# The x buffers hold x only, and the squares for the next block's norm are queued in the middle of a block

## The chip, the cores and the metric

The kernel runs on one core of a Trainium2 chip. The metric is the device time of one execution in microseconds (us); the number compared is the median of several runs. Profiles come from one profiled execution; its span runs from the first to the last instruction.

Engines are named as the profile names them: PE is TensorE (matrix products), PEld its weight loads, DVE is VectorE, ACT is ScalarE, POOL is GpSimd, and SP is the engine whose queue issues all of this kernel's DMAs.

## The reference

One layer of a streaming encoder, for a prompt of 2048 frames (behind 16 learned meta tokens) and a sample of 32 frames with a cache of 528 rows:

```
n  = rmsnorm(x, norm_g)                          # x * rsqrt(mean(x^2) + eps) * g, width 1024
q, k, v, z_a, b_g, c_g, u, z_c = split(n @ w_in) # 8 groups of 512 columns
# attention, 4 heads, chunk-causal, with relative position bias:
a  = softmax(q1 k1 / 8 + bias) - lambda * softmax(q2 k2 / 8 + bias)
o  = rmsnorm(a @ v, subln_g) * (1 - lambda_init) * silu(z_a)
# short convolution of width 3:
yc = silu(z_c) * b_g * conv3(c_g * u)
y  = rmsnorm(x + concat(o, yc) @ w_out, final_g)
```

It also returns k, v and the last two rows of the convolution's input. All of it is in 32-bit floats; the kernel splits each operand of a large product in a high and a low part and multiplies three times.

## The kernel before

The prompt is worked through in four blocks of 512 frames (p = 0 to 3); block 0 carries the meta tokens and the sample as well. For each block, x arrives transposed (features on the partitions) in eight tiles `xt`, and ScalarE and VectorE write from each a high part `xh` and a low part `xl`, already times the norm's weight (`x_load`, L141 to L174). The rest of the norm, the factor 1/sqrt(mean of squares) of each frame, is multiplied in when a projection leaves its accumulator (`rbs[p]`, L254, L280, L305, L352 and the like).

That factor is made apart. `x_stats(p + 1)` (L108) loads x once more, with the frames on the partitions, in eight tiles `xr` of 128 by 512. ScalarE squares each and sums it along its row (L115), and a few tiny instructions turn the sums into the factor r (L117, L178 to L184). `x_rms` (L121) spreads r along a diagonal (`dg`, VectorE, L127) and multiplies it with a matrix of ones (`pb`, TensorE, L129), so that every partition holds the factor of every frame; ScalarE copies that into the tile rb (L130). These three are traced at a high priority.

Within a block, four units h = 0 to 3 follow each other. `unit_a(h, p)` (L237) projects q, k, v and the gate z of one head; `attend(h, p, st)` (L432) makes the scores, softmax and outputs; `unit_c(u, p)` makes a quarter of the convolution branch. In blocks 0 to 2 no convolution unit follows h = 3. A projection is 24 products (L225) into an accumulator of the ring pj, which has two buffers; the block's first projection of q, the product `pb` and the transposes of v share that ring. Each projection's weights are loaded (`wr`), cast by ScalarE to a high part (L204) and their low part is made by GpSimd or VectorE (L78).

`unit_a` writes, in this order, the g tiles `q32`, `k32`, `v32t`, `v32`, `z32` and `l1`. The last two are written behind the last projection, z: the eviction L352 writes `z32`, and `softplus_neg` (L188 to L191) writes `l1`. The casts of k that `ev_k` makes for the score products are L285; there are two in blocks 1 to 3 and four in block 0.

Buffers come from rings of a fixed number of tiles with the same tag. The two that matter here:

- The tag xt, eight tiles of 128 by 512 (`XB = 8`). It holds the eight `xr`, the diagonal `dg`, the eight `xt`, in block 0 also the cached keys and values of the sample (`kts` and `cvt`, two per head), and in block 3 some others.
- The tag g, eight tiles of 128 by 564 (`g_tile`). It holds the short-lived tiles of the units, and later those of the output stage.

The order of the instructions on each engine and on the DMA queue isn't written out. A scheduler works it out ahead of time with a simulated timeline: at each moment an engine takes, of the instructions that are ready, the one with the highest priority, which is the one traced first unless it is marked. On the chip each engine then runs its list in that order. `x_stats(p + 1)` is traced behind `unit_a(2, p)`, and `x_rms` and `x_load(p + 1)` behind `unit_a(3, p)`:

```
st = unit_a(h, p)
if h == 2 and p < NQ - 1:
    r = x_stats(p + 1)
...
if h == H - 1 and p < NQ - 1:
    x_rms(p + 1, r)
    x_load(p + 1)
attend(h, p, st)
```

After the four blocks comes an output stage of 17 tiles (`out_first`, `out_rest`).

Of the kernel before, what the change touches and what calls it, by code (L numbers as in the profile page):

```python
# [11 lines left out]
F32 = mybir.dt.float32  # L12
# [5 lines left out]
P = 128  # L18
# [9 lines left out]
QT = 512  # L28
# [7 lines left out]
XB = 8  # L36
# [11 lines left out]
def hybrid_step(ctx: ExitStack, tc: tile.TileContext, x, xT, ckT, cv, scT, rel_bias, norm_g, w_in,  # L48
# [13 lines left out]
    one = pool("one", 1)  # L62
# [6 lines left out]
    V, S, G, T = nc.vector, nc.scalar, nc.gpsimd, nc.tensor  # L69
# [3 lines left out]
    def halved(out, a, b, op, engine=None):  # L73

        n = out.shape[-1] if len(out.shape) == 2 else out.shape[1]
        cuts = (0, n // 2, n) if engine is None and n * (out.shape[-1] if len(out.shape) > 2 else 1) > 256 else (0, n)
        for c0, c1 in zip(cuts, cuts[1:]):
            (engine or G).tensor_tensor(out[:, c0:c1], a[:, c0:c1], b[:, c0:c1], op=op)  # L78

    dma = lambda out, in_: nc.sync.dma_start(f32(out), f32(in_))  # L80
    g_tile = lambda n=564: gp.tile([P, 564], F32, tag="g", name="g")[:, :n]
# [26 lines left out]
    def x_stats(p):  # L108

        ssq = sm.tile([P, 8], F32, tag="ssq", name="ssq", bufs=1)  # L110
        for j in range(8):
            xr = one.tile([P, QT], F32, tag="xt", name="xr", bufs=XB)
            r0 = NX + QT * p + P * (j // 2)
            dma(xr, x[r0:r0 + P, 512 * (j % 2):512 * (j % 2) + 512])
            S.activation(xr, xr, AF.Square, accum_out=ssq[:, j:j + 1])  # L115
        ssp, var, r, w = (sm.tile([P, 4], F32, tag=f"x{i}", name=f"x{i}", bufs=1) for i in range(4))
        V.tensor_reduce(ssp, ssq.rearrange("p (t i) -> p t i", i=2), op=ALU.add, axis=AX.X)  # L117
        rsqrt(r, ssp, var, w, 1.0 / D)
        return r

    def x_rms(p, r):  # L121

        rb = one.tile([P, NX + QT], F32, tag="rb", name="rb")
        pb = ps_j.tile([P, 512], F32, tag="pj", name="pb")
        dg = one.tile([P, QT], F32, tag="xt", name="dg", bufs=XB)
        with tc.high_priority():
            V.tensor_tensor(by_tile(dg), ident.unsqueeze(1).broadcast_to([P, 4, P]),  # L127
                            r.unsqueeze(2).broadcast_to([P, 4, P]), op=ALU.mult)
            T.matmul(pb, lhsT=ones, rhs=dg, start=True, stop=True)  # L129
            S.copy(rb[:, :QT], pb)  # L130
        rbs[p] = rb
# [44 lines left out]
    def rsqrt(r, ssum, var, w, scale):  # L176

        V.tensor_scalar(var, ssum, scale, EPS, op0=ALU.mult, op1=ALU.add)  # L178
        S.activation(r, var, AF.Ln)
        S.activation(r, r, AF.Exp, scale=-0.5)  # L180
        V.tensor_tensor(w, r, r, op=ALU.mult)
        V.tensor_tensor(w, w, var, op=ALU.mult)
        V.tensor_scalar(w, w, -0.5, 1.5, op0=ALU.mult, op1=ALU.add)
        V.tensor_tensor(r, r, w, op=ALU.mult)  # L184
# [52 lines left out]
    def unit_a(h, p):  # L237
# [5 lines left out]
        st = {}  # L243
# [21 lines left out]
        for c in range(2):  # L265
            r, o = slice(64 * c, 64 * c + 64), slice(64 - 64 * c, 128 - 64 * c)
# [6 lines left out]
        k32 = g_tile(tw)  # L273
        ks = [ks_tile(c) for c in range(2)]
# [4 lines left out]
        def ev_k(ps, b0, b1):  # L279
            V.tensor_tensor(k32[:, b0:b1], ps, rbs[p][:, b0:b1], op=ALU.mult)  # L280
            e = min(b1, kn)
            for c in range(2):
                r, o = slice(64 * c, 64 * c + 64), slice(64 - 64 * c, 128 - 64 * c)
                d = slice(k0 + b0, k0 + e)
                S.copy(ks[c][r, d], k32[r, b0:e])  # L285
                halved(ks[c][o, d], k32[r, b0:e], f32(ks[c][r, d]), ALU.subtract)
        proj(CK + h, p, ev_k)
        dma(kT_p[h, :, k0:k0 + kn], k32[:, :kn])
        if p < NQ - 1:
# [451 lines left out]
    for p in range(NQ):  # L741
        for h in range(H):
            bz = one.tile([P, 512], F32, tag="bz", name="bz", bufs=2)
            if (h, p) != (0, 0):
                dma(bz, bzd[h])
            st = unit_a(h, p)
            if h == 2 and p < NQ - 1:
                r = x_stats(p + 1)
            if (h, p) == (0, 0):
                dma(bz, bzd[h])  # L750
            st["bz"] = bz
# [4 lines that stand above are left out]
            if p == 0:  # L756
                attend_sample(h, st)
            for u in after[p == NQ - 1][h]:
                unit_c(u, p)
# [53 lines left out]
```

## Time and profile before

| | us |
|---|---|
| median of 3 runs | 1295.74 (1294.01 to 1296.23) |
| the profiled execution | 1298.81 |
| its span | 1297.0 |
| TensorE busy | 1269.9 (98%) |
| VectorE busy | 953.9 (74%) |
| GpSimd busy | 831.4 (64%) |
| ScalarE busy | 739.1 (57%) |

The mean granted clock of TensorE is 0.994 of full speed. Block 1 begins near 250 us, block 2 near 490, block 3 near 765, and the output stage near 1050; a block hands over to the next where the `xh` and `xl` of the next one are written (rows L152 and L153).

In the profile a row of the timeline gives start, duration, engine, line, operation, output and inputs, shapes and count; in brackets stands the idle time of that engine just before and what ended it. A matrix product's duration includes its way through the array, so two products overlap, and the step from one start to the next is its cost.

### The profile page before, as it was taken

The page shows a single profiled execution, that of the slowest core. Times are in us where ns is not written, and L with a number is a line of the kernel's source. Part 1 is how long each engine was busy: PE and PEld are TensorE (multiplying, and loading weights), DVE is VectorE, ACT ScalarE, POOL GpSimd, SP SyncE. Part 2 cuts the span into 40 slices and gives each one's busy share as a digit, 9 for nine tenths or more (in the row PEclk, how much of TensorE's full clock was granted, in tenths as well). Part 3 has the DMA queues.
Part 4 walks back from the last instruction along what each step waited for, and adds up shares of the span by engine and source line. Part 5 has one row for each costly group of instructions (what it writes and reads, how often), then busy time and mean ns, then how long its engine had stood idle before and what let it go on. Part 6 is the DMA issues. An engine that isn't in the chain of part 4 may idle for free.

```text
span 1297.0 us, 21616 instructions
## 1 busy us (share of the span) xinstructions
PE 1269.9 (98%) x7058; PEld 1100.7 (85%) x7058; DVE 953.9 (74%) x2086; ACT 739.1 (57%) x1854; POOL 831.4 (64%) x1094
## 2 busy tenths in 40 slices
PE   8999999999999998999999999999999999999897
PEld 6999999988888886888888888888888888888675
DVE  7666566567888757787969678787797897756654
ACT  6655454665665457575656466665656676654322
POOL 5866767778676675486668757576777586651300
PEclk9999999999999999999999999999999999999999
DMA  9744434775444357444353453344435533556662
GB/s 284 227 125 132 140 101 116 229 235 156 123 139 133 122 154 219 150 136 139 104 170 117 141 177 110 127 138 115 124 89 157 174 112 124 182 187 226 218 192 84
DMA packets 108049, 198.75 MB, mean 153 GB/s; under 512 B 17408, under 2 KB 45600, under 8 KB 107936
## 3 DMA queue, kind: packets, MB, share of 16 engines
q1 hardware_dynamic: 107936, 197.37, 49.5%
q8 instruction: 55, 0.90, 0.3%
q14 instruction: 58, 0.48, 0.1%
HBM read 145.62 MB, written 43.26 MB: 146 GB/s over the span
## 4 chain that ended last, share of the span: by engine, by line
PE 53%; DVE 3%; DMA 3%; ACT 2%; POOL 2%; issue 1%; SPq 0%; DVEq 0%; POOLq 0%; ACTq 0%
PE pj L225 25%; PE po L693 9%; PE s L446 4%; PE s L447 3%; PE pt L462 3%; PE po L471 2%; PE po L470 2%; PE po L469 2%; DMA ct<-cat 1%; DMA out<-y 1%; PE po L685 1%; POOL cll L78 1%; DVE p L401 1%; DMA xt<-in_xT 0%; POOL wol L657 0%
## 5 line engine op out<-in xcount | busy, mean ns | idle before, releaser
L78 POOL TENSOR_TENSOR wl<-wr,wh 128x256 fp32r<-128x256 f32 x480 | 384.7, 826 | 199.0 <-ACT wh L204 186.0
L225 PE MATMUL pj<-xh,wh 128*128 128x512 f32 (+2 forms) x1280 | 456.4, 357 | 2.9 <-DVE g L352 1.2
L225 PE MATMUL pj<-xl,wh 128*128 128x512 f32 (+2 forms) x1280 | 454.9, 356 | 0.6 <-DVE xl L153 0.5
L225 PE MATMUL pj<-xh,wl 128*128 128x512 f32 (+2 forms) x1280 | 452.9, 354 | 0.0
L397 ACT ACTIVATE p<-s,nm 128x384 f32<-128x384 f32 (+5 forms) x352 | 208.8, 596 | 127.1 <-DVE nm L396 89.5
L225 PEld LDWEIGHTS pj<-xh,wh 128*128 128x128 f32 x1280 | 242.8, 190 | 34.8 <-ACT bvec L603 1.7
L225 PEld LDWEIGHTS pj<-xh,wl 128*128 128x128 f32 x1280 | 242.5, 189 | 29.9 <-issue 1.1
L225 PEld LDWEIGHTS pj<-xl,wh 128*128 128x128 f32 x1280 | 242.7, 190 | 29.2 <-DVE xl L153 1.2
L204 ACT CAST wh<-wr 128x512 fp32r<-128x512 f32 x256 | 157.4, 618 | 107.5 <-PE pj L225 81.8
L401 DVE SCALAR_TENSOR_TENSOR p<-p,cf,p 128x384 f32<-128x384 f32 (+5 forms) x176 | 155.8, 913 | 20.7 <-POOL p L400 20.3
L400 POOL TENSOR_SCALAR p<-p,cf 128x384 f32<-128x384 f32 (+5 forms) x176 | 123.4, 717 | 32.2 <-DVE cf L377 20.8
L78 POOL TENSOR_TENSOR cll<-ct,chh 128x256 fp32r<-128x256 f32 x80 | 66.7, 860 | 113.0 <-ACT chh L671 111.9
L396 DVE TENSOR_REDUCE nm<-s 128x1 f32<-128x384 f32 (+3 forms) x224 | 121.9, 558 | 17.2 <-PE s L447 16.9
L446 PE MATMUL s<-ks,q 128*128 128x384 f32 (+5 forms) x352 | 128.2, 366 | 4.8 <-ACT p L397 4.7
L466 DVE TENSOR_TENSOR al<-pt,ah 128x512 fp32r<-128x512 f32 x144 | 97.2, 683 | 39.2 <-ACT ah L465 39.0
L447 PE MATMUL s<-ks,q 128*128 128x384 f32 (+5 forms) x352 | 123.6, 353 | 0.0
L465 ACT CAST ah<-pt 128x512 fp32r<-128x512 f32 x144 | 80.4, 587 | 56.7 <-PE pt L462 50.3
L462 PE MATMUL pt<-ident,p 128*128 128x128 f32 x544 | 87.1, 273 | 1.0 <-DVE p L401 0.9
L393 DVE CUSTOM_DVE_ANT_0 s<-s,bz 128x512 f32<-128x512 f32 (+5 forms) x128 | 74.1, 588 | 15.1 <-PE s L447 12.2
L470 PE MATMUL po<-al,vh 128*128 128x256 f32 x288 | 83.5, 290 | 0.9 <-DVE al L466 0.7
L469 PE MATMUL po<-ah,vh 128*128 128x256 f32 x288 | 81.2, 282 | 0.0
L471 PE MATMUL po<-ah,vl 128*128 128x256 f32 x288 | 81.1, 282 | 0.0
(237 smaller groups left out, 2196.8 us busy)
## 6 DMA issues: line engine op xcount, KB each, us to landing
wr<-in_w_in SPq DMA_DIRECT2D x128, 512.0 KB, 3.7
ct<-cat SPq DMA_DIRECT2D x28, 512.0 KB, 4.6
q<-q SPq DMA_DIRECT2D x64, 128.0 KB, 3.0
out<-y SPq DMA_DIRECT2D x32, 256.0 KB, 4.0
ks<-ksd SPq DMA_DIRECT2D x8, 776.0 KB, 5.5
xr<-in_x SPq DMA_DIRECT2D x24, 256.0 KB, 5.1
out<-g SPq DMA_DIRECT2D x24, 256.0 KB, 3.2
xt<-in_xT SPq DMA_DIRECT2D x24, 256.0 KB, 4.6
```

The costliest lines, as they stand in the source:

```text
L78: (engine or G).tensor_tensor(out[:, c0:c1], a[:, c0:c1], b[:, c0:c1], op=op)
L204: S.copy(wh, wi)
L225: T.matmul(ps, lhsT=a[:, k % 4], rhs=b[k][:, b0:b1], start=(k == 0 and i == 0), stop=(k == KT - 1 and i == 2))
L396: V.tensor_reduce(nm[:, c, j:j + 1], s, op=ALU.min, axis=AX.X)
L397: S.activation(pr[j][c], s, AF.Exp, bias=nm[:, c, j:j + 1], scale=-1.0, accum_out=l[:, c, j:j + 1])
L400: G.tensor_scalar(a0, a0, cf[:, 0, j:j + 1], 1.0, op0=ALU.mult, op1=ALU.mult)
L401: V.scalar_tensor_tensor(a0, a1, cf[:, 1, j:j + 1], a0, op0=ALU.mult, op1=ALU.add)
L446: T.matmul(ps, lhsT=qd[c][0][:, qs], rhs=ks[c][:, col:col + w], start=True, stop=False)
L447: T.matmul(ps, lhsT=qd[c][1][:, qs], rhs=ks[c][:, col:col + w], start=False, stop=True)
L462: T.transpose(pt[:, i, P * qi:P * (qi + 1)], cols(aa[qi], NM + P * (2 * j + i), P), ident)
L470: T.matmul(po, lhsT=vh[:, kt], rhs=al[:, i], start=False, stop=False)
L693: T.matmul(ps, lhsT=a[k][:, :rows], rhs=b[k], start=(k == 0 and i == 0), stop=(k == KT - 1 and i == 2))
```

## The change

Three places change. The diagonal `dg` is taken from the ring g rather than from xt. `ev_k` keeps its last cast of k under the name `late`. And `x_stats` is traced inside `tc.issue_after(st["late"].ins)`: every instruction that it puts on ScalarE (the eight squares and the two activations of the inverse root) is queued behind that cast of unit h = 2. The order is one of issue on ScalarE alone; nothing waits for a semaphore, and the DMAs and VectorE's instructions of `x_stats` are not bound by it.

```diff
@@ x_rms
         pb = ps_j.tile([P, 512], F32, tag="pj", name="pb")
-        dg = one.tile([P, QT], F32, tag="xt", name="dg", bufs=XB)
+        dg = g_tile(QT)
         with tc.high_priority():
@@ unit_a, ev_k
                 d = slice(k0 + b0, k0 + e)
-                S.copy(ks[c][r, d], k32[r, b0:e])
+                st["late"] = S.copy(ks[c][r, d], k32[r, b0:e])
                 halved(ks[c][o, d], k32[r, b0:e], f32(ks[c][r, d]), ALU.subtract)
@@ the loop over blocks
             if h == 2 and p < NQ - 1:
-                r = x_stats(p + 1)
+                with tc.issue_after(st["late"].ins):
+                    r = x_stats(p + 1)
```

## The prediction

> **What bounds the kernel now.** I read the page first, then the waits of TensorE by stretch, then the chain of waits through the one stretch that loses time.
>
> ```profile
> span 1297.0 us, 21616 instructions
> PE 1269.9 (98%) x7058; PEld 1100.7 (85%) x7058; DVE 953.9 (74%) x2086; ACT 739.1 (57%) x1854; POOL 831.4 (64%) x1094
> ```
>
> TensorE is busy 98% of the span, so an edit on other engines can win only where TensorE waits: 27 us in all, or where its clock is low. The waits of TensorE between 480 and 530 us, where block 1 hands over to block 2 (us in total, times, longest):
>
> ```profile
> PE s L446 <- ACT p L397: 4.5, 2, 2.8
> PE pj L225 <- DVE g L352: 1.0, 1, 1.0
> PE pj L225 <- ACT rb L130: 0.5, 1, 0.5
> PE pt L462 <- DVE p L401: 0.3, 1, 0.3
> ```
>
> That is 6.3 us of idle TensorE in one place, and it is followed by a lowered clock. Busy time by stretch (stretch, its length, PE, PEld, DVE, ACT, POOL, granted clock, DMA share, GB/s):
>
> ```profile
> 260.00:270.00 10.00, 10.00 (x50) 8.34 (x50) 7.73 (x22) 8.59 (x24) 5.18 (x7) 1.00 0.69 225
> 350.00:400.00 50.00, 50.00 (x269) 43.18 (x268) 41.41 (x92) 31.01 (x79) 39.71 (x51) 1.00 0.49 143
> 490.00:500.00 10.00, 8.50 (x37) 6.43 (x36) 5.07 (x12) 5.50 (x16) 1.85 (x2) 1.00 1.03 329
> 510.00:515.00 5.00, 2.90 (x11) 1.58 (x9) 4.93 (x13) 2.47 (x6) 4.77 (x6) 0.89 0.81 247
> 515.00:520.00 5.00, 2.33 (x9) 2.06 (x10) 4.59 (x13) 3.00 (x10) 4.80 (x8) 0.50 0.99 311
> 520.00:525.00 5.00, 5.00 (x15) 3.96 (x15) 3.72 (x9) 1.53 (x4) 1.59 (x3) 0.59 0.97 329
> 765.00:770.00 5.00, 5.00 (x23) 3.96 (x22) 4.88 (x10) 5.00 (x11) 3.26 (x4) 1.00 0.27 96
> ```
>
> Elsewhere TensorE is full: after the hand-over 0 to 1 (260 to 270), in the middle of a block (350 to 400), and in the hand-over 2 to 3 (765 to 770). Only the hand-over 1 to 2 is broken. Its chain of waits (start, us, what):
>
> ```profile
> 487.62 6.22 DMA xt<-in_xT
> ...
> 493.93 0.73 ACT xh L152
> ...
> 495.53 0.63 ACT xr L115
> ...
> 503.32 0.61 ACT xr L115 x2
> ...
> 504.46 0.52 ACT wh L204
> ...
> 507.38 0.88 POOL p L400
> ...
> 516.84 0.79 ACT p L397 x2
> ```
>
> The reader should see one line of dominoes. The last x load of block 2 is issued only at 487.62, ScalarE waits for it until 493.93, then runs the eight squares for block 3 (xr, L115) between its weight casts and exponentials until 504, and everything behind is late until TensorE gets its scores at 517.
>
> **Part one: the squares move.** A square is an activation and a read of its accumulator:
>
> ```profile
> L115 ACT ACTIVATE xr<-xr x24: 614/632/642, 27.9 to 503.2; 128x512 f32<-128x512 f32 x24
> L115 ACT ACTIVATION_READ_ACCUMULATOR xr<-xr x24: 185/188/203, 28.5 to 503.7; 128x1 f32 x24
> ```
>
> Their work is at most 8 x (632 + 188) ns = 6.6 us of ScalarE per block, in three blocks; nothing is removed, it moves. The new place is behind the last copy of k in unit h = 2, for example here in block 1:
>
> ```profile
> 384.78 1.27 ACT L285 CAST ks<-g 64x512 fp32r<-64x512 f32 x2
> ```
>
> There ScalarE is busy 31 of 50 us (row 350 to 400), so 19 us are free and 6.6 fit; behind the squares stand weight casts and exponentials, and TensorE waits for those. I cost the move at 0: the squares at the hand-over 0 to 1, in a busier ScalarE (8.59 of 10), cost TensorE nothing. If that cover fails, the bound is all three sets, 3 x 6.6 = 20 us. The order is on ScalarE alone: the loads of the squares (eight DMAs) are not held and go out as slots come free, at the hand-over, as now (seven of them in one row):
>
> ```profile
> 489.34 7.27 SPq L80 DMA_DIRECT2D xr<-in_x  x7
> ```
>
> They then sit in the eight x slots until mid-block, and the eight transposed loads follow the squares there instead of just after the hand-over. That takes up to 2 MB out of the stretch 515 to 520, whose DMA share is 0.99, to one at 0.49 (eight loads of this row of the page's DMA issues, with KB and us to landing).
>
> ```profile
> xt<-in_xT SPq DMA_DIRECT2D x24, 256.0 KB, 4.6
> ```
>
> In block 0 the slots are shared with the cached keys and values, so squares come later in pairs; half of ScalarE is free there too, and I put 0.
>
> **Part two: the diagonal leaves the x slots.** In the old order it sits in one of the eight until its product is made, so the last x load of a block waits for a slot until the hand-over (487.62 above). After the change all eight can be in beforehand: ScalarE's wait up to 493.93 goes. With the squares gone too, I take both of the first idle times that hang on this chain (4.5 and the 0.5 at rb, whose copy stood behind the squares) as removed: 5.0 us. With them goes the low clock: 0.9 us after 514.09 at half (0.45), 2.33 x 0.50 = 1.17, and 5 x 0.41 = 2.05, together 3.7. The gain is 5.0 + 3.7 = **8.7 us**. It can be 0, if something else is just as late, and at most 10.0 with the other two waits (1.0 and 0.3).
>
> But the diagonal enters another ring, and this speaks against the change. The ring g hands its slots out in program order: in the output stage the load of the next y (g) is never issued before the square (also g) that is traced ahead of it, though slots are free. Two pairs of ScalarE and of the load queue:
>
> ```profile
> 1101.41 0.62 ACT L695 ACTIVATE g<-g 128x512 f32<-128x512 f32 x1
> ...
> 1111.59 0.63 ACT L695 ACTIVATE g<-g 128x512 f32<-128x512 f32 x1 [2.70 <-DVE g L694]
> ```
> ```profile
> 1101.60 0.43 SPq L80 DMA_DIRECT2D g<-in_x  x1
> ...
> 1112.02 0.36 SPq L80 DMA_DIRECT2D g<-in_x  x1
> ```
>
> So the diagonal, made early today, must wait for the last g tile of unit h = 3, l1, whose first write is L188, behind the eviction L352:
>
> ```profile
> 247.70 0.30 DVE L188 TENSOR_SCALAR g<-g 128x272 f32<-128x272 f32 x1
> ...
> 490.88 0.68 DVE L352 TENSOR_TENSOR g<-pj,rb 128x512 f32<-128x512 f32 x1
> ...
> 493.67 0.41 DVE L188 TENSOR_SCALAR g<-g 128x512 f32<-128x512 f32 x1
> ...
> 765.12 0.69 DVE L352 TENSOR_TENSOR g<-pj,rb 128x512 f32<-128x512 f32 x1 [0.22 <-PE pj L225]
> ...
> 766.66 0.41 DVE L188 TENSOR_SCALAR g<-g 128x512 f32<-128x512 f32 x1
> ```
> ```profile
> L127 DVE TENSOR_TENSOR dg<-ident,x x3: 691/691/1186, 59.6 to 514.2; 128x512 f32<-128x512 f32 x3
> ```
>
> And its product pb holds its turn in the ring pj, so that the next block's first projection stands behind it. Today it does not; pb comes before that projection's first matmul without a wait (two matmuls per row, then the projection's first):
>
> ```profile
> 488.26 1.02 PE L129 MATMUL pb<-dg,ones 128*128 128x512 f32 x2
> ...
> 491.61 0.50 PE L225 MATMUL pj<-xh,wh 128*128 128x512 f32 x1 [1.01 <-DVE g L352]
> ...
> 514.09 0.59 PE L446 MATMUL s<-ks,q 128*128 128x272 f32 x1 [1.74 <-ACT p L397]
> ...
> 765.10 1.02 PE L129 MATMUL pb<-dg,ones 128*128 128x512 f32 x2
> ...
> 767.29 0.39 PE L225 MATMUL pj<-xh,wh 128*128 128x512 f32 x1
> ```
>
> In the hand-over 1 to 2 the diagonal would be ready at 493.67 + 0.41 + 0.69 = 494.77, against the projection's 491.61: 3.2 us late. If L188 follows L352 at once it is 490.88 + 0.68 + 0.41 + 0.69 = 492.66, 1.05 late. I take the middle, 2.1. In 2 to 3 it is 766.66 + 0.41 + 0.69 = 767.76 against 767.29, 0.5 late, or not at all with L188 at once; I take 0.5. In 0 to 1 the first L188 stands at 247.70, before the products: 0. (The time of pb itself only changes sides.) TensorE can fill these waits with scores of the heads under way, so the cost lies between 0 and 3.7; I take **2.6**.
>
> **The sum.** Against the profiled execution, 1298.81 us (span 1297.0 and 1.81 around it): -8.7 + 2.6 = -6.1, 1292.7. That execution is 3.07 above the median of the three runs, so the median goes from 1295.74 to **1289.6**.
>
> **Rivals.**
> *A, the new wait is filled.* The scores under way cover it, as TensorE was covered in 765 to 770. Then -8.7: 1287.0.
> *B, a new wait in the old place.* In 1 to 2 the projection waits the full 3.2 us, the clock drops again and takes 3.7, and 2 to 3 pays 0.5: 7.4 of the 8.7 come back, 1294.4, no change. For it: a wait of 1.74 us (at 514.09) was followed by a granted clock of 0.50; against it: the wait of 1.01 (at 491.61) left it at 1.00 (row 490 to 500). The Trainium skill, TensorE: Matmul & The Clock Gate, section What's actually happening, says that the array falls to half clock after an idle window of about 3.4 us, the window running free of the program. This case's trace shows the low clock after a wait of 1.74 us; by that rule a wait of 3.2 us would mostly keep the clock, and B would end near 1290.7.
> *C, slower.* The diagonal's wait costs both later hand-overs 3.2 us and a drop of the clock: 2 x 6.9 = 13.8, less 8.7, is +5.1: 1300.8. It decides from a total of 8.7, that is, once both waits pass the 1.0 that was harmless. For it: order in the ring g as shown. Against: in 2 to 3 VectorE is only 0.5 late and TensorE was full.
> *D, it does not do what it says.* The order only sets an earliest place; the squares may be queued far behind it, even near the hand-over, and the chain stays: 1295.7. Against it: 19 us of 50 free on ScalarE.
>
> **How the numbers follow.** About 0.2% (2.6 us) is what a measurement of this kernel can tell from no change. Forecast 0.42, A 0.16, B 0.18, C 0.15, D 0.09. Faster is the forecast and A: 0.58. Same is B and D: 0.27. Slower is C: 0.15. The forecast's own range is 1285.7 to 1290.7, from a gain of 10.0 with no new wait to one of 8.7 with the full 3.7. The range of the whole reaches from a gain of 10.0 and 1.7 more, 1284.0, which I allow for what a new order may win of the span's other idle (27.1 - 6.3 = 20.8 us), up to just short of C, 1299.5.
>
> **What would show it.** Right: no row L115 near a hand-over; the last xt load issued mid-block in blocks 1 and 2; the clock 1.00 all through 480 to 530; TensorE idle there under 3 us; dg (L127) right behind L188. Wrong: dg made early (then ring g is not in order, and the price falls on the conv units, whose tiles share it); a wait on pb or dg followed by a low clock; TensorE waits in the middle of h = 2 behind L115; a new idle stretch anywhere else, since the order of all queues is worked out anew.

## The result, and the profile after

The changed kernel takes 1310.92 us (median of 6 runs, 1307.34 to 1314.63) against 1296.26 us for the kernel before on the same chip: a ratio of 1.0118, interval 1.0106 to 1.0129. It is 14.7 us slower where 6.1 us faster was forecast, and lies outside the range. The profiled execution took 1314.63 us, the longest of the six; over the six the mean clock goes from 0.988 (this one) to 0.994 (the shortest).

The head of the page of the changed kernel (busy time, share of the span, instructions):

```profile
span 1312.8 us, 21644 instructions
PE 1278.3 (97%) x7058; PEld 1106.5 (84%) x7058; DVE 948.6 (72%) x2086; ACT 741.0 (56%) x1854; POOL 822.6 (63%) x1094
```

TensorE is idle for 1312.8 - 1278.3 = 34.5 us, where it was 27.1. Its mean granted clock over the span is 0.988, before 0.994, and span x (1 - clock) gives 15.8 us lost to a low clock, before 7.8 (the clock has three decimals, so such a figure is good to some 0.7 us). The span grew by 1312.8 - 1297.0 = 15.8 us, which in this execution is half idle time (7.4) and half low clock (8.0); what is left of the span is 1262.5 against 1262.1. The work is the same; the waits and the clock are not.

Where it went is read from busy time by stretch (stretch, its length, PE, PEld, DVE, ACT, POOL, granted clock, DMA share, GB/s). The changed kernel:

```profile
325.00:345.00 20.00, 18.30 (x88) 15.14 (x88) 15.22 (x43) 11.26 (x33) 11.19 (x17) 0.91 0.36 116
385.00:415.00 30.00, 26.68 (x127) 22.36 (x126) 20.99 (x45) 20.92 (x55) 20.15 (x28) 0.89 0.73 226
495.00:515.00 20.00, 17.77 (x65) 13.54 (x64) 18.09 (x44) 14.20 (x34) 10.92 (x14) 0.83 0.69 238
765.00:785.00 20.00, 16.85 (x65) 12.72 (x64) 17.20 (x33) 14.68 (x33) 7.80 (x9) 0.83 0.45 148
```

Three of the same stretches in the kernel before (the hand-over 1 to 2 stands in the prediction):

```profile
325.00:345.00 20.00, 20.00 (x108) 17.18 (x107) 17.08 (x47) 13.73 (x37) 10.42 (x15) 1.00 0.44 135
385.00:415.00 30.00, 30.00 (x172) 26.35 (x171) 23.33 (x58) 18.11 (x46) 21.22 (x29) 1.00 0.43 132
765.00:785.00 20.00, 20.00 (x91) 16.41 (x90) 18.64 (x35) 15.86 (x36) 15.60 (x19) 1.00 0.43 126
```

In such a row the loss of TensorE is its length less PE, plus PE x (1 - clock). The 3.5 of the old stall is the sum over its rows of 5 us from 510 on, which the prediction shows (0.3 + 1.2 + 2.0).

| place | before, us | after, us |
|---|---|---|
| hand-over 1 to 2 (before 490 to 525, after 495 to 515) | 6.3 + 3.5 = 9.8 | 2.2 + 3.0 = 5.2 |
| hand-over 2 to 3 (765 to 785) | 0 | 3.2 + 2.9 = 6.1 |
| middle of block 1, unit h = 2 (385 to 415) | 0 | 3.3 + 2.9 = 6.2 |
| block 1, unit h = 1 (325 to 345) | 0 | 1.7 + 1.6 = 3.3 |

The old stall is gone, but a new one of half its size stands in its place, the next hand-over has one that it never had, and block 1 loses time in its middle. These four make +11.0; the other 4.8 are spread over small places. The largest of them is the output stage: from 1195 to 1260 TensorE is idle for 3.3 us in both kernels, but its clock is 0.97 there (1.9 us), before 1.00.

**The two hand-overs.** The order of VectorE in the changed kernel (start, us, what), around 1 to 2, where only its ends are shown, and then around 2 to 3, where only the short reads of accumulators are left out:

```profile
500.81 0.68 DVE L352 TENSOR_TENSOR g<-pj,rb 128x512 f32<-128x512 f32 x1
...
504.49 0.41 DVE L188 TENSOR_SCALAR g<-g 128x512 f32<-128x512 f32 x1
504.82 0.68 DVE L127 TENSOR_TENSOR g<-ident,x 128x512 f32<-128x512 f32 x1
...
773.62 0.68 DVE L352 TENSOR_TENSOR g<-pj,rb 128x512 f32<-128x512 f32 x1
774.22 0.54 DVE L396 TENSOR_REDUCE nm<-s 128x1 f32<-128x384 f32 x1
774.69 0.55 DVE L393 CUSTOM_DVE_ANT_0 s<-s,bz 128x384 f32<-128x384 f32 x1
...
775.16 1.05 DVE L153 SCALAR_TENSOR_TENSOR xl<-xt,ng,xh 128x512 fp32r<-128x512 f32 x1
776.14 0.55 DVE L393 CUSTOM_DVE_ANT_0 s<-s,bz 128x384 f32<-128x384 f32 x1
...
776.61 0.47 DVE L188 TENSOR_SCALAR g<-g 128x512 f32<-128x512 f32 x1
777.01 1.21 DVE L127 TENSOR_TENSOR g<-ident,x 128x512 f32<-128x512 f32 x1
```

The diagonal (L127) stands right behind L188, as ring g would have it. But L188 starts 3.0 us behind L352 in 2 to 3 and 3.7 in 1 to 2; in the kernel before it was 1.5 and 2.8 (rows in the prediction). TensorE at the same places:

```profile
503.44 0.69 PE L446 MATMUL s<-ks,q 128*128 128x384 f32 x1 [1.98 <-ACT p L397]
...
506.17 1.91 PE L129 MATMUL pb<-g,ones 128*128 128x512 f32 x2
...
773.84 0.34 PE L447 MATMUL s<-ks,q 128*128 128x384 f32 x1
777.15 0.70 PE L446 MATMUL s<-ks,q 128*128 128x400 f32 x1 [2.97 <-ACT p L397]
...
778.36 2.05 PE L129 MATMUL pb<-g,ones 128*128 128x512 f32 x2 [0.18 <-DVE g L127]
779.42 1.42 PE L225 MATMUL pj<-xh,wh 128*128 128x512 f32 x1
```

This is not the picture that a reader expects of a late diagonal: TensorE waits for it only 0.18 us in 2 to 3, and not at all in 1 to 2. It waits 2.97 and 1.98 for an exponential, because the scores are all that it has to do: the next block's projection is behind pb, and pb is behind the diagonal. When the scores have no free tile left TensorE stands still, the clock falls (a row of 0.50 stands in the last section), and pb itself takes 2.05 us where it took 1.02. That an earlier diagonal would take this wait away is not in these rows; the experiments show it.

**The squares.** They went where the change says: all 24 in mid-block, none near a hand-over, and the eight x loads of block 2 are issued at 395.4 to 401.6 rather than up to 487.62 (groups of two tiles, the second for 370 to 520 alone: ns min/median/max, first and last start):

```profile
L115 ACT ACTIVATE xr<-xr x24: 612/616/634, 152.2 to 667.4; 128x512 f32<-128x512 f32 x24
...
L80 SPq DMA_DIRECT2D xt<-in_xT x8: 328/382/505, 395.4 to 401.6; - x8
```

What stands around the eight squares of block 1, the timelines of ScalarE (first and second square, then the one instruction among them), VectorE and TensorE in order of time:

```profile
394.66 0.63 ACT L115 ACTIVATE xr<-xr 128x512 f32<-128x512 f32 x1
...
395.29 0.62 ACT L115 ACTIVATE xr<-xr 128x512 f32<-128x512 f32 x1
...
397.56 2.67 DVE L401 SCALAR_TENSOR_TENSOR p<-p,cf,p 128x272 f32<-128x272 f32 x3 [2.12 <-POOL p L400]
...
397.74 0.62 ACT L428 ACTIVATE o<-o 128x512 f32<-128x512 f32 x1
...
400.16 1.21 DVE L429 SCALAR_TENSOR_TENSOR o<-o,g 128x512 f32<-128x512 f32 x1
401.29 0.68 DVE L305 TENSOR_TENSOR g<-pj,rb 128x512 f32<-128x512 f32 x1
...
402.03 1.12 PE L316 MATMUL ptv<-ident,g 128*128 128x128 f32 x4 [3.32 <-DVE g L305]
```

TensorE waits 3.32 us for the eviction L305, which stands behind L401 (late by GpSimd) and L429 on VectorE. L429 needs the exponential L428, which is queued among the squares; it was done at 398.36, so here the squares are near the chain without being its last link. L429 starts when L401 is done, and L401 had waited for GpSimd.

### The profile page after: what moved, and what is told of

It is laid out like the page before. It is cut to its first block, busy times and chain, and to the rows that moved or that the text cites. A ratio compares the mean times of both kernels' runs of the same rounds, so it can differ in the third digit from the quotient of the medians.

```text
span 1312.8 us, 21644 instructions
## 1 busy us (share of the span) xinstructions
PE 1278.3 (97%) x7058; PEld 1106.5 (84%) x7058; DVE 948.6 (72%) x2086; ACT 741.0 (56%) x1854; POOL 822.6 (63%) x1094
## 4 chain that ended last, share of the span: by engine, by line
PE 52%; DVE 5%; DMA 2%; ACT 2%; issue 1%; POOL 0%; DVEq 0%; ACTq 0%; POOLq 0%
PE pj L225 25%; PE po L693 10%; PE s L446 3%; PE s L447 3%; PE pt L462 3%; PE po L469 2%; PE po L470 2%; PE po L471 2%; DVE p L401 1%; DMA ct<-cat 1%; PE po L685 1%; ACT p L397 1%; DVE nm L396 1%; DVE xl L153 0%; DMA out<-y 0%
## 5 line engine op out<-in xcount | busy, mean ns | idle before, releaser
L78 POOL TENSOR_TENSOR wl<-wr,wh 128x256 fp32r<-128x256 f32 x480 | 377.8, 811 | 207.5 <-ACT wh L204 196.5
L401 DVE SCALAR_TENSOR_TENSOR p<-p,cf,p 128x384 f32<-128x384 f32 (+5 forms) x176 | 155.2, 910 | 28.0 <-POOL p L400 27.7
L78 POOL TENSOR_TENSOR cll<-ct,chh 128x256 fp32r<-128x256 f32 x80 | 62.5, 807 | 110.6 <-ACT chh L671 110.6
```

What stands on the lines that cost most here:

```text
L401: V.scalar_tensor_tensor(a0, a1, cf[:, 1, j:j + 1], a0, op0=ALU.mult, op1=ALU.add)
```

## The experiments

Each part alone first, then the diagonal's lateness and the squares' placing by themselves. The loss columns are worked out as above, from the span, the PE row and the mean clock of each page; each ratio is against the kernel before, run on the same chip beside it. The loss columns come from one profiled execution, which lies up to 3.9 us from the median (e9_mix 3.0 below it, e12_mix_late 2.0 above): they say where time went, and small differences in them say nothing.

| kernel | squares | diagonal | median us | ratio (interval) | idle | low clock |
|---|---|---|---|---|---|---|
| e0_neutral | hand-over | as before | 1295.36 | 0.9993 (0.9984 to 1.0003) | 26.2 | 5.2 |
| e1_squares_only | mid-block | as before | 1297.92 | 1.0013 (1.0004 to 1.0023) | 26.2 | 3.9 |
| e2_dg_only | hand-over | ring g | 1311.04 | 1.0113 (1.0098 to 1.0128) | 37.2 | 10.5 |
| e3_dg_ahead | mid-block | ring g, handed out early | 1300.47 | 1.0030 (1.0020 to 1.0039) | 29.2 | 3.9 |
| e11_first_write_high | mid-block | ring g | 1311.55 | 1.0127 (1.0104 to 1.0150) | 34.9 | 15.8 |
| e7_loads_first_only | hand-over | x ring, behind the loads | 1310.02 | 1.0104 (1.0089 to 1.0120) | 36.5 | 7.8 |
| e8_late_diag | hand-over | as e7, queued behind L188 | 1313.87 | 1.0130 (1.0105 to 1.0154) | 39.4 | 13.1 |
| e4_dg_after_loads | mid-block | x ring, behind the loads | 1299.95 | 1.0019 (1.0006 to 1.0032) | 28.6 | 5.2 |
| e5_spread | 3, 3, 2 in three units | as e4 | 1296.91 | 1.0004 (0.9995 to 1.0013) | 27.2 | 3.9 |
| e9_mix | mid-block | x ring; behind the loads from block 2 on | 1294.66 | 0.9995 (0.9984 to 1.0006) | 23.3 | 2.6 |
| e12_mix_late | mid-block | e9, queued behind L188 | 1304.36 | 1.0066 (1.0049 to 1.0083) | 30.1 | 11.7 |
| e10_mix_small_squares | mid-block, 16 columns | e9 | 1293.16 | 0.9984 (0.9974 to 0.9993) | 24.3 | 2.6 |
| e13_mix_squares_back | hand-over | e9 | 1301.98 | 1.0053 (1.0038 to 1.0068) | 29.0 | 10.4 |
| e6_mix_spread | 3, 3, 2 in three units | e9 | 1290.75 | 0.9958 (0.9943 to 0.9973) | 22.0 | 3.9 |

In all of them span less idle less low clock is 1261.7 to 1265.9, so most of what moved, moved in these two columns. The main theory, the first where the expectations number them, is that the late diagonal costs the time; the rivals are the squares' new place, the slot that the diagonal takes in ring g, and the new order as such.

**e0_neutral: a new order without the change.** A copy of one column per block on ScalarE, traced ahead of each block's first unit, gives the scheduler a reason to write another order.

```diff
+            if (h, p) == (0, 0):
+                tick = const.tile([P, 1], F32, name="tick")
+            if h == 0:
+                S.copy(tick, rbs[p][:, :1])
             st = unit_a(h, p)
```

> The kernel before plus one copy of a single column on ScalarE at the start of each block (four in all, under 0.3 us each, result unused). The scheduler then works out another order for every queue, with the work the same. Theory 3 (any new order costs some us by chance): several us away from the kernel before, to either side, with small waits of TensorE in new places. Theories 1 and 2 (the changed kernel's loss has named places): within 3 us of the kernel before.

No difference, but the test is smaller than it was meant to be. Up to about 540 us the order on TensorE is nearly that of the kernel before (163 of its 171 rows from 480 to 530 stand in the same order), so the stall at 1 to 2 stayed (6.05 us idle in 490 to 530). From there to about 1080 us the order is another one, and no time is lost by it: the stretch 755 to 795 has 0.1 us of idle time. One new order of blocks 2 and 3 is therefore no cause of 15 us by itself; blocks 0 and 1 are not tested.

**e1_squares_only: part one alone.** The changed kernel with the diagonal back in the x slots.

```diff
-        dg = g_tile(QT)
+        dg = one.tile([P, QT], F32, tag="xt", name="dg", bufs=XB)
```

> The squares are queued in mid-block as in the changed kernel, but the diagonal stays in the x ring, so it is made early again. Theory 1 (the late diagonal in ring g is what costs): the hand-over 2 to 3 is full again and the kernel is faster than the kernel before, near 1290. Theory 2 (eight squares in a row in mid-block cost TensorE time in unit h = 2): TensorE waits behind L305 after the squares in block 1, the clock drops there, and the time is at or above the kernel before, 1296 to 1303.

2.0 us slower: nearly nothing. It halves the stall at 1 to 2 (3.0 idle and 1.5 low clock in 490 to 530, from 9.8) but does not gain by it; block 1 loses 0.8 us in the middle and 1.0 from 325 to 345, where it lost nothing. In the middle of block 1 the squares show as a link of a chain. VectorE there:

```profile
397.92 0.16 DVE L117 TENSOR_REDUCE x<-ssq 128x4 f32<-128x8 f32 x1 [2.24 <-ACT xr L115]
398.00 0.68 DVE L305 TENSOR_TENSOR g<-pj,rb 128x512 f32<-128x512 f32 x1
```

The small sum over the eight squares (L117) is queued ahead of the eviction L305 and holds VectorE for 2.24 us until the last square is done; TensorE, waiting for L305, stands 0.8 us.

**e2_dg_only: part two alone.** The kernel before with the diagonal in ring g.

```diff
-        dg = one.tile([P, QT], F32, tag="xt", name="dg", bufs=XB)
+        dg = g_tile(QT)
```

> The diagonal comes from ring g, the squares stay where they were before the change. Theory 1: dg is made right behind L188 at each hand-over, TensorE waits for it at 1 to 2 and 2 to 3, and the time is 1300 to 1308. Theory 2: no loss from the diagonal, 1294 to 1297.

The whole loss, 15.1 us, without a single square moved. TensorE at the hand-over 1 to 2:

```profile
500.51 0.69 PE L446 MATMUL s<-ks,q 128*128 128x384 f32 x1 [6.13 <-ACT p L397]
```

The old cause (squares among the exponentials) and the new one (nothing else to do until pb, which follows at 501.31) meet in one wait of 6.13 us. The middle of block 1 loses nothing here (30.00 of 30 us, clock 1.00).

**e3_dg_ahead: ring g, but early.** The changed kernel with the diagonal taken from ring g and written before unit h = 3 is traced; its product stays where it was.

```diff
+            if h == H - 1 and p < NQ - 1:
+                dg = x_diag(r)     # g_tile(QT) and the multiply of x_rms
             st = unit_a(h, p)
...
-                x_rms(p + 1, r)
+                x_rms(p + 1, dg)
```

> The changed kernel with one line moved: the diagonal still comes from ring g but is traced ahead of unit h = 3, so it is made before that unit's g tiles and not behind l1. Theory 1: the waits at the hand-overs go, 5 to 9 us faster than the changed kernel, 1302 to 1306 or less; dg stands some 15 us ahead of L352. Theory 2: the mid-block wait behind the squares stays and most of the loss with it, 1305 to 1311.

10.4 of the 14.7 us come back. Windows of this kernel, both hand-overs and the middle of block 1:

```profile
385.00:415.00 30.00, 26.72 (x133) 22.50 (x132) 22.03 (x49) 22.75 (x62) 19.50 (x27) 0.94 0.72 234
495.00:515.00 20.00, 19.00 (x86) 15.23 (x85) 17.46 (x40) 14.96 (x36) 12.01 (x16) 1.00 0.70 230
765.00:785.00 20.00, 20.00 (x90) 16.42 (x89) 19.43 (x35) 15.92 (x37) 14.94 (x18) 1.00 0.39 120
```

The two hand-overs lose 1.0 us together in these rows (2.1 with all of 490 to 530), where the changed kernel lost 11.3; the middle of block 1 still loses 3.3 + 1.6 = 4.9, of 6.2. So the hand-overs belong to the diagonal's lateness, and most of the middle does not.

**e11_first_write_high: L188 sooner, a miss.** The changed kernel with the first write of l1 given high priority, in the hand-over's unit alone.

```diff
+    def softplus_neg(out, z, first=False):
...
+        if first:
+            with tc.high_priority():
+                V.tensor_scalar(out, z, -1.0, 40.0, op0=ALU.mult, op1=ALU.min)
...
```

> The changed kernel with one priority raised: the first write of l1 (L188) in unit h = 3 of blocks 0 to 2 comes at high priority, so that the diagonal behind it in ring g is made about 1 us after L352 instead of 4. Theory 1 (lateness at the hand-over): the hand-over 2 to 3, which lost 6 us, loses 0 to 2, and the kernel is 4 to 8 us faster than the changed kernel, 1303 to 1307. Theory 1 wrong: within 2 us of the changed kernel.

The order between L352 and L188 did not change, so it amounts to the changed kernel run once more, and gives the same time (1311.55). Whether a sooner L188 would help isn't answered by it.

**e7_loads_first_only and e8_late_diag: lateness without ring g, a first try.** In e7 the kernel before traces the x loads ahead of the diagonal, so that the x ring hands the diagonal a slot last. e8 is e7 with the diagonal's one instruction on VectorE also queued behind the first L188 of the unit (`st["l1"]`, which `ev_z` keeps; those lines are left out).

```diff
-                x_rms(p + 1, r)
                 x_load(p + 1)
+                x_rms(p + 1, r)
```
```diff
...
                 x_load(p + 1)
+                with tc.issue_after(st["l1"].ins):
+                    x_rms(p + 1, r)
```

> The kernel before with two lines swapped: the x loads are traced ahead of the diagonal, which takes the slot that the first x tile frees. The last x load no longer waits for the diagonal; the squares stay at the hand-over. Theory 1a: dg is ready before L352 at every hand-over, so no loss: 1290 to 1297. Theory of the removed chain (the late load alone is worth 3.6 us of ScalarE): the stall at 1 to 2 shrinks, 1289 to 1293. Rival (the diagonal is still too late there): 1298 or more.

> The kernel before, with the diagonal in the x ring behind the eight x loads instead of ahead of them, and its one instruction on VectorE queued behind the first write of l1 (L188) of unit h = 3. The ring g is not touched; only the lateness is added. Theory 1a (it is the lateness): the loss of the diagonal in ring g comes back without ring g, 1304 to 1312, with TensorE waiting for dg at 1 to 2 and 2 to 3. Theory 1b (it is the slot taken from ring g): near its sister without the late order, within 3 us.

e8 is as slow as the change, but e7 is nearly so (13.9 us), hence the pair tells little: 3.9 us between them. e7 makes the diagonal late at another place, the hand-over 0 to 1, where the loads have to wait for the squares' slots. Its waits of TensorE between 245 and 285 (us in total, times, longest), which the kernel before does not have:

```profile
PE ptv L316 <- DVE g L305: 2.6, 1, 2.6
PE pb L129 <- DVE dg L127: 2.5, 1, 2.5
```

**e4_dg_after_loads and e5_spread: the squares' place.** e4 is e7 with the squares in mid-block, as the change has them; in e5 three, three and two of them follow the last copy of k in the units h = 0, 1 and 2 instead of all eight in h = 2.

```diff
...
-            if h == 2 and p < NQ - 1:
+            if h < 3 and p < NQ - 1:
                 with tc.issue_after(st["late"].ins):
-                    r = x_stats(p + 1)
+                    r = x_stats(p + 1, ((0, 1, 2), (3, 4, 5), (6, 7))[h])
```

> The changed kernel with the diagonal in the x ring behind the eight loads: squares in mid-block, all eight loads early, dg not behind l1. Theory 1: all of the loss is gone and the forecast of the prediction is met, 1288 to 1294. Theory 2 (the squares in mid-block give back what the hand-over wins): 1294 to 1299, like the kernel with the squares alone moved.

> As the kernel with the diagonal behind the loads, with the squares in three groups (3, 3, 2) behind the casts of k of units h = 0, 1 and 2 instead of eight behind that of h = 2. Theory 2 (eight in a row delay what is queued behind them): the waits behind L305 in mid-block shrink, 2 to 5 us faster than with the eight together. Theory 2 wrong: the same within 2 us.

With the squares away from the hand-over the same trace order costs 3.8 us instead of 13.9, and spreading them takes another 3.0. In e5 TensorE is full from 385 to 415 (30.00 of 30 us, clock 1.00). Both still wait 2.5 us for the diagonal at 0 to 1.

**e9_mix and e12_mix_late: lateness alone, on a clean base.** e9 mends that last wait: for block 1 the diagonal is traced ahead of the loads, for blocks 2 and 3 behind them. e12 is e9 with the diagonal of blocks 2 and 3 queued behind L188. The diagonal stays in the x ring in both, so ring g is untouched.

```diff
...
+                if p == 0:
+                    x_rms(p + 1, r)
                 x_load(p + 1)
+                if p > 0:
+                    with tc.issue_after(st["l1"].ins):   # e12 only
+                        x_rms(p + 1, r)
```

> Squares in mid-block as in the changed kernel; the diagonal in the x ring, ahead of the x loads for block 1 and behind them for blocks 2 and 3. The kernel with it behind the loads everywhere waited 2.5 us for it at 0 to 1 and lost 3 more just after. Theory 1: those 5 us are gone, 1293 to 1296. If the loss after 250 us has nothing to do with the diagonal: 1298 to 1301.

> The mixed kernel (squares in mid-block; the diagonal in the x ring, ahead of the loads for block 1 and behind them for blocks 2 and 3), with one edge more: for blocks 2 and 3 the diagonal's one instruction is queued behind the first write of l1 (L188). Ring g is not touched. Theory 1a (lateness alone): TensorE waits for pb at 1 to 2 and 2 to 3 with a low clock behind, 1300 to 1308, and 0 to 1 unchanged. Theory 1b (ring g's slot): within 3 us of the mixed kernel, 1292 to 1298.

This pair decides it: 1294.66 against 1304.36, or 0.9995 against 1.0066 of the kernel before, which are 9 to 10 us for one instruction that is queued late, with the order that follows from it. VectorE of e9 at the hand-over 2 to 3:

```profile
757.20 1.11 DVE L127 TENSOR_TENSOR dg<-ident,x 128x512 f32<-128x512 f32 x1
...
760.71 0.68 DVE L352 TENSOR_TENSOR g<-pj,rb 128x512 f32<-128x512 f32 x1
...
763.72 0.48 DVE L188 TENSOR_SCALAR g<-g 128x512 f32<-128x512 f32 x1
```

and the windows of e9, then of e12:

```profile
495.00:515.00 20.00, 19.93 (x92) 16.57 (x93) 18.77 (x48) 13.84 (x35) 13.55 (x18) 1.00 0.74 228
765.00:785.00 20.00, 18.13 (x83) 14.75 (x83) 18.26 (x38) 12.30 (x31) 14.92 (x20) 1.00 0.40 118
```

```profile
495.00:515.00 20.00, 19.68 (x79) 15.06 (x78) 16.76 (x51) 12.12 (x34) 9.88 (x14) 0.83 0.54 178
765.00:785.00 20.00, 16.87 (x63) 12.66 (x62) 16.74 (x37) 12.57 (x31) 12.63 (x16) 0.83 0.22 60
```

TensorE of e12 at the two places (this kernel's line numbers are one higher from L192 on):

```profile
494.70 0.44 PE L447 MATMUL s<-ks,q 128*128 128x384 f32 x1 [1.96 <-ACT p L398]
...
768.54 0.70 PE L447 MATMUL s<-ks,q 128*128 128x400 f32 x1 [2.94 <-ACT p L398]
...
769.76 2.04 PE L129 MATMUL pb<-dg,ones 128*128 128x512 f32 x2 [0.19 <-DVE dg L127]
```

L188 follows L352 by the same 3.0 us in e9; there it gates nothing, because the diagonal is 3.5 us ahead of L352. With the diagonal behind L188, e12 repeats the changed kernel's waits to a few hundredths: 1.96 at 1 to 2 for 1.98, and 2.94 and 0.19 at 2 to 3 for 2.97 and 0.18. It loses 0.3 + 3.3 and 3.1 + 2.9 us in these two windows, and the 1.96 ahead of the first, where e9 loses 0.1 and 1.9. The slot in ring g, as a thing of its own, is not needed to explain these waits.

Two things go beyond the hand-overs. In the profiled executions, which are 14.6 us apart, e12 also loses some 5 us more than e9 in the output stage (1195 to 1260), and no run shows why. And e12 is some 6.6 us faster than the changed kernel, which has the same lateness and the squares in the same place: the two stretches of block 1, 325 to 345 and 385 to 415, lose 1.7 us in e12 and 9.5 in the changed kernel. For that part of the loss ring g does matter.

**e10_mix_small_squares: the squares' work itself.** e9 with each square over 16 of its 512 columns (scaled up), so that most of the sum is left out. A form over a single column gave no time.

```diff
-            S.activation(xr, xr, AF.Square, accum_out=ssq[:, j:j + 1])
+            S.activation(xr[:, :16], xr[:, :16], AF.Square, scale=32.0 ** 0.5, accum_out=ssq[:, j:j + 1])
```

> As the mixed kernel, but each of the 24 squares reads 16 columns, scaled up, instead of 512; the sums are then estimates and the outputs of blocks 1 to 3 differ. All loads and the order rule stay. It prices the squares where they stand. Theory 2 (in mid-block they cost TensorE time): 2 to 6 us faster than the mixed kernel, 1288 to 1292. Free there: within 1.5 us of it.

1.5 us less than e9 (1293.16 against 1294.66), but the two intervals overlap, so a cost of the squares' work is not shown; the ends of the intervals allow up to some 4 us. The middle of block 1 (385 to 415) still loses 1.0 us here, as e9 loses 0.8: the loss there isn't the time that the squares take.

**e13_mix_squares_back: the diagonal's trace order alone.** The kernel before with only e9's order of diagonal and loads; the squares stay at the hand-over. Against e9:

```diff
-                with tc.issue_after(st["late"].ins):
-                    r = x_stats(p + 1)
+                r = x_stats(p + 1)
```

> The kernel before with the mixed order of the diagonal and nothing else: the squares stay at the hand-over. If the move of the squares is what relieves 1 to 2: the stall there stays near 8 to 10 us and the time at 1294 to 1298. If the late x load was the greater part of that stall: 1290 to 1293, as good as with the squares moved.

1301.98: 6.7 us slower than the kernel before and 7.3 slower than e9. So moving the squares is worth 7.3 us once the diagonal is well placed, while in e1, with the diagonal as before, it was worth nothing. The stall at 1 to 2 does shrink here (2.1 idle and 1.5 low clock in 490 to 530), but a wait of 3.0 us for an exponential appears in 2 to 3, as in e7. Why it does is not settled.

**e6_mix_spread: both put right.** e9 with the squares spread as in e5.

```diff
-            if h == 2 and p < NQ - 1:
+            if h < 3 and p < NQ - 1:
...
+                if p == 0:
+                    x_rms(p + 1, r)
                 x_load(p + 1)
+                if p > 0:
+                    x_rms(p + 1, r)
```

> The mixed order of the diagonal, with the squares in three groups (3, 3, 2) behind the casts of k of units h = 0, 1 and 2. Theories 1 and 2 together: the 5 us at 0 to 1 gone from the spread kernel, 1290 to 1293, faster than the kernel before. If either theory is short: 1294 to 1298.

1290.75 us (1287.80 to 1290.90), 0.9958 of the kernel before (0.9943 to 0.9973): 0.4% faster than the kernel before, and 3.9 us faster than e9. Its windows:

```profile
325.00:345.00 20.00, 20.00 (x108) 17.14 (x107) 16.55 (x42) 12.83 (x35) 10.70 (x16) 1.00 0.50 160
385.00:415.00 30.00, 30.00 (x171) 26.15 (x170) 26.35 (x65) 19.92 (x54) 23.07 (x33) 1.00 0.51 155
495.00:515.00 20.00, 20.00 (x100) 16.80 (x99) 18.78 (x47) 14.93 (x39) 16.46 (x23) 1.00 0.75 221
765.00:785.00 20.00, 18.67 (x85) 14.96 (x84) 18.46 (x38) 12.45 (x32) 17.75 (x24) 1.00 0.38 110
```

TensorE is full in three of the four stretches where the change lost time, and the clock is 1.00 in all four. Where the 3.9 us against e9 sit is not shown: the profiled executions of the two are only 0.8 us apart.

## Why the prediction was wrong, step by step

**The stall at 1 to 2 and its 8.7 us: right.** The chain was read rightly, a late x load, then squares among the exponentials. With both causes gone and the diagonal early, 490 to 530 loses 2.1 us (e3) or 0.3 (e9) where it lost 9.8. Each cause alone takes away about half or a little more: 4.5 us are left in e1, 3.6 in e13.

**The diagonal behind L188: right.** It was read from how ring g hands out slots in the output stage, and the trace has L127 0.33 and 0.40 us behind the start of L188 in the two later hand-overs. At 0 to 1 it cost nothing, as forecast: the stretch 245 to 285 has 1.0 us of idle time in the changed kernel (0.2 before), and that is a wait for xh, not for pb.

**What that wait costs: wrong, and it turns the gain at the hand-overs into a loss.** The prediction took 2.6 us with an upper bound of 3.7 (2.1 or at most 3.2 for 1 to 2, and 0.5 for 2 to 3). The two hand-overs lost 5.2 + 6.1 = 11.3. Three things in that step failed.

1. It took the distance from L352 to L188 out of the kernel before. In 2 to 3 that distance is 3.0 us in place of 1.5, since a reduction, two bias passes and one xl of 1.05 us now stand between. The order around the new dependency was written anew, so the old distance was no bound.
2. It measured lateness against the first matmul of the projection and let scores fill the rest. Scores do not fill it: they ran out, and TensorE waited 1.98 and 2.97 us for exponentials, while pb itself waited only 0.18.
3. It left the clock at 1.00. The clock loss is 3.0 and 2.9 us, about half of the 11.3. The low-clock rows of 1 to 2 were in the prediction (3.7), but only rivals B and C carried them over to the new wait.

With 9.8 gone and 11.3 come, the hand-overs are 1.5 us worse in place of the 6.1 better of the sum. The price of the lateness in whole kernels is of the same size: 9.7 us in e12 against e9, 10.4 in e3 against the changed kernel.

**A term that the sum did not have: block 1.** The sum of part two is for the hand-overs alone, and there it is short by 11.3 - 2.6 = 8.7. The rest of the loss, 9.5 us in the two stretches of block 1 and 4.8 in small places, stands at nothing in it; only the list of what would show it wrong names waits in the middle of h = 2 and a new idle stretch elsewhere. The two stretches of block 1 lose 1.8 us where the squares alone move (e1), 1.6 where the diagonal alone goes to ring g (e2), 1.7 with the squares moved and a late diagonal in the x ring (e12), but 6.6 in e3 and 9.5 in the changed kernel, which have both the squares in mid-block and the diagonal in ring g. So the greater part of it takes the two parts of the change together. By which wait ring g brings it about is not shown. As a whole, part two was put at 2.6 us, and the changed kernel is 13.0 us slower than e1, which lacks only this part.

**The squares at 0: wrong, by less.** Moved alone (e1) they make the kernel 2.0 us slower, and in the middle of block 1 they stop TensorE for 0.8 us through L117. Spreading them wins 3.0 (e5 against e4) and 3.9 (e6 against e9). Average room on ScalarE, 19 free us of 50, was the wrong cover to name: the wait in e1 comes from what VectorE has queued behind the last square, and with most of the squares' work gone (e10) the middle still loses 1.0.

**The rivals.** C was the nearest: the diagonal's wait at both later hand-overs with a drop of the clock, from waits of over 1.0. Its size per hand-over, 6.9, is close to the 5.2 and 6.1 measured. Its total of 1300.8 was still 10 us short, although its hand-overs came out dearer (+5.1) than measured (+1.5), because no rival had a loss away from them (9.5 in the two stretches of block 1, 4.8 in small places). A, B and D fall: the wait was not filled, it was not in one place alone, and the squares did move. The argument against C was that TensorE was full in 2 to 3 and the diagonal only 0.5 us late there; a full stretch of the old order said nothing about the new one.

**What stays open.** Why the squares in mid-block and the diagonal in ring g together cost what neither costs alone in block 1; the idle time of the output stage, 1195 to 1260, which goes from 1.7 (e1) to 6.1 us (e8), and in some kernels takes a low clock with it, without an order that any run explains; and the wait at 2 to 3 in e7 and e13.

## What to carry to other kernels

A small tile on the way to the next block's first matmul should not be handed out behind tiles that are written late: the ring hands out slots in program order, so before moving such a tile, look up which tile is handed out just ahead of it and when that one is first written. Price a late gate by what the in-order engine still has behind it, with the clock drop in the price, and do not bound it with distances from the old order, for the order can be written anew around a new dependency. Two edits that look apart can cost together what neither costs alone, so try each by itself and both. Here work that fills gaps did better in small portions: over three blocks, eight squares at once cost 3.0 and 3.9 us more than the same eight in three portions.

## What the runs showed of the hardware

**The clock does not go by the length of a wait alone.** In the changed kernel a wait of 1.98 us, ending at 503.44, was followed by a granted clock of 0.50 from 505 to 510:

```profile
500.00:505.00 5.00, 3.02 (x12) 2.15 (x10) 5.00 (x10) 4.32 (x10) 2.89 (x4) 0.84 1.06 351
505.00:510.00 5.00, 4.75 (x10) 3.15 (x10) 4.39 (x15) 3.92 (x13) 0.00 (x0) 0.50 0.93 346
```

In e7 the longer wait of 2.48 us at 0 to 1 left it at 1.00, there and in the 10 us that follow:

```profile
250.00:260.00 10.00, 7.52 (x37) 5.93 (x36) 9.68 (x25) 8.85 (x24) 4.96 (x6) 1.00 0.68 217
```

The Trainium skill, TensorE: Matmul & The Clock Gate, section What's actually happening, says that the gate looks at a window of about 3.4 us that runs free of the program. That the window runs free would fit these two places, since a wait can fall within one window or across two whatever its length; no run here tests it. The Trainium skill, in the same section, puts the low clock after at least one such window of idleness. That does not agree: a wait of 1.98 us is shorter than such a window.

**Squares overlap the read of their accumulator.** They start 0.63 us apart (394.66 and 395.29), so eight in a row take about 4.9 us; the 6.6 of the prediction had added the two durations.
